# Where the state scan of a hybrid decoder runs: VectorE in two chains, or GpSimd in one

## The chip, the core and the metric

The kernel runs on one core of one Trainium2 chip. The metric is the device time of one execution in microseconds, the median of several runs. Five engines work side by side, each through its own queue in order: TensorE (PE; its weight loads are PEld), VectorE (DVE), ScalarE (ACT), GpSimd (POOL), and SyncE (SP), which only issues DMAs here.

## The reference

Two decoder layers over 256 positions of width 2048, in float32. Each layer projects the normed input, runs sliding-window attention and a state space model (S5) side by side, merges them through gates, and adds a gated feed-forward block. What matters here is the state space branch: 64 groups with 64 complex states each, advanced along the positions.

```python
def s5_ssm(u, lam_re, lam_im, log_dt, b_re, b_im, c_re, c_im, d_skip):
    ...
    bu_r = jnp.einsum('blgh,gph->blgp', uf, bbar_r)
    bu_i = jnp.einsum('blgh,gph->blgp', uf, bbar_i)
    ...
    _, _, s_r, s_i = lax.associative_scan(combine, (a_r, a_i, bu_r, bu_i), axis=1)
    y = (jnp.einsum('blgp,ghp->blgh', s_r, c_re) - jnp.einsum('blgp,ghp->blgh', s_i, c_im) + d_skip * uf)
    return y.reshape(B, L, SSM_WIDTH)
```

So s[t] = a * s[t-1] + (B u)[t] in complex numbers, a fixed for each state.

## The kernel before, in words

**Weights.** The kernel streams 475 MB of weights in pieces of up to 512 KB (128 x 4 x 256 numbers). The class Weights loads a piece by DMA, ScalarE rounds it to a high part `whi` (L106), VectorE forms the remainder `wlo = w - whi` (L121), and TensorE multiplies both parts with the activations (L295): 16 matmuls a piece, 8 with 512 columns and 8 with 256. High parts are made three pieces ahead, low parts two.

**The order of the work** is written out by hand. Every piece is one tick of the class Clock; side jobs are put on ticks with `later`, `at` and `stages`, and issued there into the queues of their engines. An engine works off its queue in order, so a waiting instruction holds up all behind it on that engine.

**The state space branch.** Two groups make a pair, whose 2 x 64 states fill 128 partitions; there are 32 pairs, real and imaginary. Two positions are joined into one step, so 256 positions give 128 columns c of the tile `S[128, 2, 32, 128]` (real/imaginary, pair, column). `states_in` (L735 to L748) fills all of S with the inputs of the steps, in eight ticks up to tick 37 (layer 0) and 24 (layer 1); ScalarE copies them out of PSUM (L748). Then `scan` (L759) makes 127 steps in place: for each column c, four products of the coefficients `scan_c` with column c - 1, and two sums into column c, for the real and the imaginary factor in turn. These are spread over ticks 39 to 109 in layer 0 and 26 to 109 in layer 1, one or two steps to a tick, in VectorE's queue between the `wlo` subtractions and the evictions. VectorE does each step in two halves of 16 pairs (two products at L766, four adds at L769), so that the two halves take turns.

**What uses the result.** At tick 110 `channels` starts: its matmuls `ys` (L963) read all columns of S. Their other operands `cb` and `ca` are cleared by GpSimd (L927, L928, issued at tick 91) and filled by ScalarE (L933, ticks 92 and 93).

**Other work in the same ticks.** Attention (`normed`, `attend`), the gate evictions (L343, L344, L896, L916, L943), and the weight stream. GpSimd has little: memsets of `prepare` (L649, L678), those of `cb` and `ca`, and a sum of squares at the very start (L412).

Of the kernel before, what the change touches and what calls it, by code (L numbers as in the profile page):

```python
# [10 lines left out]
F32 = mybir.dt.float32  # L11
# [7 lines left out]
P = 128  # L19
# [148 lines left out]
def build(ctx, tc, a, out):  # L168
    nc = tc.nc
    v, s, g, pe = nc.vector, nc.scalar, nc.gpsimd, nc.tensor  # L170
# [5 lines left out]
    tmp = ctx.enter_context(tc.tile_pool(name="tmp", bufs=1))  # L176
# [6 lines left out]
    def nm(x):  # L183
        uid[0] += 1
        return f"{x}_{uid[0]}"
# [372 lines left out]
    scan_c = cst.tile([P, L, 2, 2, 32], F32, name="scan_c")  # L558
# [146 lines left out]
    def layer(l, norm):  # L705
# [51 lines left out]
            at(v0 + n, states_in, n)  # L757

        def scan(first, last):  # L759

            S = hold["S"]
            for c in range(first, last):
                prs = [tmp.tile([P, 2, 2, 16], F32, name=nm("sc"), tag="sc", bufs=4) for _ in range(2)]
                fs = (slice(0, 16), slice(16, 32))
                for pr, f in zip(prs, fs):
                    v.tensor_mul(pr, scan_c[:, l, :, :, f], S[:, :, f, c - 1].unsqueeze(1).to_broadcast([P, 2, 2, 16]))  # L766
                for r in range(2):
                    for pr, f in zip(prs, fs):
                        v.tensor_add(S[:, :, f, c], S[:, :, f, c], pr[:, :, r, :])  # L769


        def c_times_a():
# [17 lines left out]
        for n in range(s0, s1):  # L790
            c = [1 + (P - 1) * (m - s0) // (s1 - s0) for m in (n, n + 1)]
            at(n, scan, *c)
# [389 lines left out]
```

## Time and profile before

| | |
|---|---|
| median of 3 runs | 2632.5 us (2630.88 to 2633.15) |
| the profiled execution's own time | 2632.42 us |
| its span | 2630.5 us |
| mean granted TensorE clock | 0.994 |
| busy: PE, PEld, DVE, ACT, POOL | 99%, 86%, 73%, 48%, 1% |
| HBM | 181 GB/s over the span |

The span is the time between the first and the last instruction of the profiled execution; its own time is 1.9 us longer. Matmuls overlap in their pipeline, so a busy PE need not be PE at its peak. The page also gives a chain of waits: from the last instruction back to what released each one. L numbers are lines of the kernel. A time in a stretch counts overlapping instructions once.

### The profile page before, as it was taken

The page shows a single profiled execution, that of the slowest core. Times are in us where ns is not written, and L with a number is a line of the kernel's source. Part 1 is how long each engine was busy: PE and PEld are TensorE (multiplying, and loading weights), DVE is VectorE, ACT ScalarE, POOL GpSimd, SP SyncE. Part 2 cuts the span into 40 slices and gives each one's busy share as a digit, 9 for nine tenths or more (in the row PEclk, how much of TensorE's full clock was granted, in tenths as well). Part 3 has the DMA queues.
Part 4 walks back from the last instruction along what each step waited for, and adds up shares of the span by engine and source line. Part 5 has one row for each costly group of instructions (what it writes and reads, how often), then busy time and mean ns, then how long its engine had stood idle before and what let it go on. Part 6 is the DMA issues. An engine that isn't in the chain of part 4 may idle for free.

```text
span 2630.5 us, 40564 instructions
## 1 busy us (share of the span) xinstructions
PE 2591.1 (99%) x15716; PEld 2259.7 (86%) x15716; DVE 1932.4 (73%) x3648; ACT 1267.8 (48%) x1725; POOL 29.0 (1%) x34
## 2 busy tenths in 40 slices
PE   7999899999999999999999999999999999999999
PEld 6878788888888888888888788888888888888888
DVE  8889997866765666566677999887666656665664
ACT  5666545544443444334455675465544434443442
POOL 2000000000000000000000000000000000000000
PEclk9999999999999999999999999999999999999999
DMA  6544455666655565566664445556656556655655
GB/s 203 169 129 144 145 170 164 200 209 194 203 172 191 190 189 179 192 199 187 199 201 160 141 149 170 178 173 211 213 185 187 183 199 188 190 186 187 188 180 172
DMA packets 139825, 477.85 MB, mean 182 GB/s; under 512 B 14960, under 2 KB 25456, under 8 KB 139632
## 3 DMA queue, kind: packets, MB, share of 16 engines
q1 hardware_dynamic: 139488, 475.06, 56.4%
q8 instruction: 123, 2.02, 0.3%
q14 instruction: 70, 0.57, 0.1%
q10 hardware_dynamic: 144, 0.20, 0.0%
HBM read 471.01 MB, written 4.19 MB: 181 GB/s over the span
## 4 chain that ended last, share of the span: by engine, by line
PE 81%; DVE 14%; ACT 3%; issue 1%; DMA 0%; SPq 0%; ACTq 0%; DVEq 0%
PE acc L295 79%; DVE wlo L121 5%; DVE S L769 3%; DVE sc L766 2%; ACT whi L106 1%; DVE wh L344 1%; DVE scs L855 1%; PE v L746 1%; PE ys L963 1%; ACT scs L869 1%; DVE ga L896 0%; DVE ga L916 0%; DMA w<-in_w_in 0%; PE acc L323 0%; PE bt L672 0%
## 5 line engine op out<-in xcount | busy, mean ns | idle before, releaser
L106 ACT CAST whi<-w 128x1024 fp32r<-128x1024 f32 (+1 forms) x881 | 910.6, 1047 | 769.6 <-PE acc L295 606.4
L121 DVE TENSOR_TENSOR wlo<-w,whi 128x1024 fp32r<-128x1024 f32 (+1 forms) x881 | 1061.4, 1219 | 221.2 <-ACT whi L106 220.2
L295 PE MATMUL acc<-h,whi 128*128 128x512 f32 x4448 | 1128.6, 396 | 0.8 <-DVE wh L344 0.8
L295 PEld LDWEIGHTS acc<-h,whi 128*128 128x128 f32 x4448 | 802.3, 189 | 156.8 <-issue 9.4
L295 PEld LDWEIGHTS acc<-h,wlo 128*128 128x128 f32 x4448 | 606.1, 190 | 53.5 <-DVE wlo L121 10.9
L295 PE MATMUL acc<-h,wlo 128*128 128x256 f32 x4448 | 621.8, 283 | 5.3 <-DVE wlo L121 5.3
L295 PE MATMUL acc<-hid,whi 128*128 128x512 f32 x1384 | 346.6, 392 | 0.0
L295 PEld LDWEIGHTS acc<-hid,whi 128*128 128x128 f32 x1384 | 248.9, 189 | 44.5
L337 DVE TENSOR_REDUCE j<-acc 128x512 f32<-128x1024 f32 x88 | 107.8, 1225 | 134.4 <-PE acc L295 134.4
L295 PEld LDWEIGHTS acc<-hid,wlo 128*128 128x128 f32 x1384 | 188.8, 190 | 13.5
L295 PE MATMUL acc<-hid,wlo 128*128 128x256 f32 x1384 | 193.0, 282 | 0.0
L1102 DVE TENSOR_TENSOR xn<-xn,acc 128x512 f32<-128x512 f32 x47 | 32.3, 688 | 173.5 <-PE acc L295 173.5
L769 DVE TENSOR_TENSOR S<-S,sc 128x32 f32<-128x32 f32 x1016 | 153.5, 222 | 0.0
L295 PE MATMUL acc<-mg,whi 128*128 128x512 f32 x512 | 128.2, 392 | 0.0
L766 DVE TENSOR_TENSOR sc<-scan_c,S 128x64 f32<-128x64 f32 x508 | 115.6, 269 | 0.0
L295 PEld LDWEIGHTS acc<-mg,whi 128*128 128x128 f32 x512 | 92.1, 189 | 16.5
L295 PE MATMUL acc<-yg,whi 128*128 128x512 f32 x384 | 96.2, 392 | 0.0
L295 PEld LDWEIGHTS acc<-yg,whi 128*128 128x128 f32 x384 | 69.1, 189 | 12.3
L295 PE MATMUL acc<-ya,whi 128*128 128x512 f32 x256 | 68.5, 410 | 10.0 <-DVE ya L161 6.0
L295 PEld LDWEIGHTS acc<-mg,wlo 128*128 128x128 f32 x512 | 69.8, 190 | 5.0
L351 ACT CAST hid<-j 128x512 fp32r<-128x512 f32 x44 | 27.4, 623 | 96.9 <-DVE j L1072 96.9
L295 PE MATMUL acc<-mg,wlo 128*128 128x256 f32 x512 | 71.4, 282 | 0.0
(238 smaller groups left out, 1500.7 us busy)
## 6 DMA issues: line engine op xcount, KB each, us to landing
w<-in_w_fi SPq DMA_DIRECT2D x352, 512.0 KB, 4.3
w<-in_w_in SPq DMA_DIRECT2D x207, 512.0 KB, 3.7
w<-in_w_fo SPq DMA_DIRECT2D x176, 512.0 KB, 4.4
w<-in_w_out SPq DMA_DIRECT2D x64, 512.0 KB, 4.4
w<-in_w_ab SPq DMA_DIRECT2D x32, 512.0 KB, 3.5
w<-in_w_sb SPq DMA_DIRECT2D x32, 512.0 KB, 4.1
w<-in_w_glu SPq DMA_DIRECT2D x16, 512.0 KB, 3.8
x<-in_x SPq DMA_DIRECT2D x8, 256.0 KB, 5.8
```

Of the source, the lines that this page charges most:

```text
L106: self.nc.scalar.copy(part[0][:, f, :], w[:, f, :])
L121: self.nc.vector.tensor_sub(lo[:, f, :], w[:, f, :], hi[:, f, :].bitcast(F32))
L295: pe.matmul(o, w, r, start=start, stop=last and j == m - 1 and lo_part == 1, skip_group_check=True)
L337: v.tensor_reduce(t, ps.rearrange("p s (a t) -> p s t a", a=2), axis=AX.X, op=ALU.add)
L344: v.tensor_add(t, t, ps[:, :, :T])
L351: s.copy(hi, src)
L746: pe.matmul(pss[r][:, c0 : c0 + P], bt[ri][o : o + 64, 2 * q4 + i, :], ur[o : o + 64, 2 * q4 + i, :], start=True, stop=True)
L766: v.tensor_mul(pr, scan_c[:, l, :, :, f], S[:, :, f, c - 1].unsqueeze(1).to_broadcast([P, 2, 2, 16]))
L769: v.tensor_add(S[:, :, f, c], S[:, :, f, c], pr[:, :, r, :])
L855: v.tensor_tensor_reduce(scs[b][:, f, :], scs[b][:, f, :], pv[:, f, :], 1.0, sk[:, b : b + 1], ALU.add, ALU.max, accum_out=mx[:, b, n : n ...
L869: s.activation(z, z, AF.Copy, scale=rd[:, b, n : n + 1])
L1102: v.tensor_add(t, t, ps[:, :, :T])
```

## The change

The scan's products and sums are issued on GpSimd (`g`) and no longer on VectorE (`v`), and each covers all 32 pairs: one product of 2 x 2 x 32 elements a partition and two adds of 2 x 32, where there were two products of 64 and four adds of 32. The product tile has two buffers. Where the steps stand among the ticks is not changed.

```diff
         def scan(first, last):
-
             S = hold["S"]
             for c in range(first, last):
-                prs = [tmp.tile([P, 2, 2, 16], F32, name=nm("sc"), tag="sc", bufs=4) for _ in range(2)]
-                fs = (slice(0, 16), slice(16, 32))
-                for pr, f in zip(prs, fs):
-                    v.tensor_mul(pr, scan_c[:, l, :, :, f], S[:, :, f, c - 1].unsqueeze(1).to_broadcast([P, 2, 2, 16]))
+                pr = tmp.tile([P, 2, 2, 32], F32, name=nm("sc"), tag="sc", bufs=2)
+                g.tensor_mul(pr, scan_c[:, l], S[:, :, :, c - 1].unsqueeze(1).to_broadcast([P, 2, 2, 32]))
                 for r in range(2):
-                    for pr, f in zip(prs, fs):
-                        v.tensor_add(S[:, :, f, c], S[:, :, f, c], pr[:, :, r, :])
+                    g.tensor_add(S[:, :, :, c], S[:, :, :, c], pr[:, :, r, :])
```

## Rows read from the trace of the kernel before

**Rows 1.** The page: busy time, share of the span and instructions of each engine, and the chain that ended last, its shares by engine and by line.
```profile
PE 2591.1 (99%) x15716; PEld 2259.7 (86%) x15716; DVE 1932.4 (73%) x3648; ACT 1267.8 (48%) x1725; POOL 29.0 (1%) x34
...
PE 81%; DVE 14%; ACT 3%; issue 1%; DMA 0%; SPq 0%; ACTq 0%; DVEq 0%
PE acc L295 79%; DVE wlo L121 5%; DVE S L769 3%; DVE sc L766 2%; ACT whi L106 1%; DVE wh L344 1%; DVE scs L855 1%; PE v L746 1%; PE ys L963 1%; ACT scs L869 1%; DVE ga L896 0%; DVE ga L916 0%; DMA w<-in_w_in 0%; PE acc L323 0%; PE bt L672 0%
```

**Rows 2.** Busy time by stretch, all engines: the two scan stretches, and one of 20 us in which nothing disturbs the weight loop. Columns: stretch, its length, busy us (and instructions) of each engine, granted clock, DMA share, GB/s.
```profile
150.00:402.00 252.00, 237.81 (x1420) 198.45 (x1423) 246.82 (x992) 144.11 (x278) 3.63 (x2) 0.97 0.48 151
1422.00:1696.00 274.00, 268.06 (x1642) 228.47 (x1641) 268.85 (x1017) 161.84 (x299) 3.63 (x2) 0.99 0.52 162
...
1340.00:1360.00 20.00, 20.00 (x116) 17.62 (x115) 13.92 (x20) 12.42 (x18) 0.00 (x0) 1.00 0.64 203
```

**Rows 3.** The same view for the matmuls of the weight loop (L295) alone: PE, PEld.
```profile
150.00:402.00 252.00, 214.79 (x1152) 180.66 (x1151) 0.97 0.48 151
...
1422.00:1696.00 274.00, 245.79 (x1354) 210.48 (x1353) 0.99 0.52 162
```

**Rows 4.** The timeline, in order of time: the last copy into S, the last adds of the scan and the first matmuls that read S, first of layer 0 and then of layer 1. Columns: start us, us, engine, line, operation, out<-in, count, idle time before and what ended it.
```profile
147.03 1.07 ACT L748 COPY S<-v 128x512 f32<-128x512 f32 x2 [2.06 <-PE v L746]
...
399.32 3.57 PE L963 MATMUL ys<-S,cb 128*32 128x127 f32 x64 [2.06 <-DVE S L769]
399.59 0.59 DVE L769 TENSOR_TENSOR S<-S,sc 128x32 f32<-128x32 f32 x4
...
1417.31 1.08 ACT L748 COPY S<-v 128x512 f32<-128x512 f32 x2 [1.59 <-PE v L746]
...
1693.90 0.60 DVE L769 TENSOR_TENSOR S<-S,sc 128x32 f32<-128x32 f32 x4
1693.97 1.98 PE L963 MATMUL ys<-S,cb 128*32 128x127 f32 x64
```

**Rows 5.** VectorE's groups by line and shape in 150 to 402 us, and below the "..." that ends them, two of 1422 to 1696 us. Columns: line, engine, operation, names, shapes, count | busy us, mean ns of one | idle time before.
```profile
L121 DVE TENSOR_TENSOR wlo<-w,whi 128x1024 fp32r<-128x1024 f32 x73 | 88.8, 1217 | 1.0 <-ACT whi L106 1.0
L769 DVE TENSOR_TENSOR S<-S,sc 128x32 f32<-128x32 f32 x508 | 76.7, 221 | 0.0
L766 DVE TENSOR_TENSOR sc<-scan_c,S 128x64 f32<-128x64 f32 x254 | 57.8, 269 | 0.0
...
L896 DVE TENSOR_TENSOR ga<-wh,rms 128x512 f32<-128x512 f32 x8 | 5.5, 692 | 0.3
L916 DVE TENSOR_TENSOR ga<-ga,wh 128x512 f32<-128x512 f32 x8 | 5.5, 692 | 0.3
L943 DVE TENSOR_TENSOR gs<-gs,rms 128x512 f32<-128x512 f32 x5 | 3.5, 693 | 0.2
...
L809 DVE SCALAR_TENSOR_TENSOR q<-q,qg,qrs 128x512 f32<-128x512 f32 x2 | 1.5, 752 | 0.1
...
L375 DVE SCALAR_TENSOR_TENSOR qrs<-rs,rs 128x512 f32<-128x512 f32 x2 | 1.4, 692 | 0.1
...
L121 DVE TENSOR_TENSOR wlo<-w,whi 128x1024 fp32r<-128x1024 f32 x85 | 103.4, 1217 | 0.2 <-issue 0.2
...
L809 DVE SCALAR_TENSOR_TENSOR q<-q,qg,qrs 128x512 f32<-128x512 f32 x4 | 3.0, 752 | 0.1
```

**Rows 6.** The timeline of 19 to 26 us: GpSimd's adds of 512 elements, each reading the sum of the one before, and VectorE's instructions beside the last of them. Columns as in rows 4.
```profile
19.58 1.27 POOL L412 TENSOR_TENSOR ssq<-ssq,sq 128x512 f32<-128x512 f32 x1
20.92 1.27 POOL L412 TENSOR_TENSOR ssq<-ssq,sq 128x512 f32<-128x512 f32 x1
...
23.54 1.21 DVE L121 TENSOR_TENSOR wlo<-w,whi 128x1024 fp32r<-128x1024 f32 x1
23.61 2.27 POOL L412 TENSOR_TENSOR ssq<-ssq,sq 128x512 f32<-128x512 f32 x1
...
24.68 1.27 DVE L455 TENSOR_SCALAR cw<-cw 128x64 f32<-128x64 f32 x1
```

**Rows 7.** GpSimd's other operations: two of the timeline (columns as in rows 4; the second reads what the first wrote), and two groups by line and shape (columns as in rows 5).
```profile
2.09 0.24 POOL L268 IOTA ndist<- 128x128 f32 x1
2.40 0.29 POOL L270 TENSOR_SCALAR_AFFINE_SELECT ndist<-ndist 128x128 f32<-128x128 f32 x1
...
L649 POOL MEMSET pw<- 128x2048 f32 x4 | 7.1, 1816 | 317.2 <-PE acc L295 317.2
...
L678 POOL MEMSET k<- 128x1024 f32 x2 | 1.9, 963 | 0.0
```

**Rows 8.** The timeline near 36 us, when GpSimd is idle: a VectorE product of 64 neighbouring elements a partition.
```profile
35.88 0.22 DVE L569 TENSOR_TENSOR cw<-params,cw 128x64 f32<-128x64 f32 x1
```

**Rows 9.** The timeline of layer 0: GpSimd's memset of `cb` and ScalarE's first copies into it.
```profile
259.28 1.81 POOL L927 MEMSET cb<- 128x2048 f32 x1 [227.64 <-PE sc L850]
...
342.56 2.51 ACT L933 COPY cb<-cc 64x512 f32<-64x512 f32 x4
```

**Rows 10.** TensorE by the microsecond around a wait of layer 0. Columns: stretch, its length, PE busy us (and matmuls), granted clock, DMA share, GB/s.
```profile
280.00:281.00 1.00, 0.37 (x2) 1.00 0.04 16
...
283.00:284.00 1.00, 0.00 (x0) 0.75 0.68 164
284.00:285.00 1.00, 0.82 (x2) 0.50 0.70 279
...
290.00:291.00 1.00, 1.00 (x8) 0.83 0.64 66
```

## The prediction

> **What bounds the kernel now.** I first read the busy line and the chain that ended last [rows 1]: TensorE is busy nearly all the time, yet the chain also passes through VectorE, the two scan lines L766 and L769 among it. A mean hides where, so I next cut the span into stretches. The scan of layer 0 lies in 150 to 402 us and that of layer 1 in 1422 to 1696 us; there VectorE is busy for 246.8 of 252 us and 268.9 of 274 us, while GpSimd does two memsets [rows 2]. So VectorE is full in the two scan stretches, and only there.
>
> What would TensorE need alone? In an undisturbed stretch it does 116 matmuls of the weight loop in 20 us [rows 2]. The 1152 and 1354 of L295 [rows 3] then take 198.6 and 233.4 us. The other matmuls add 237.8 - 214.8 = 23.0 us and 268.1 - 245.8 = 22.3 us [rows 2, 3]. The floors are 221.6 and 255.7 us against 252 and 274: a scan that vanished could give back 30.4 + 18.3, nearly 49 us, and no more.
>
> The scan ends as it is needed: in layer 0 the last add ends at 400.2 us, and the first `ys` matmul had waited 2.06 us for the scan; in layer 1 the end is at 1694.5 us. The states are complete far earlier, when the last copy into S ends: 148.1 and 1418.4 us [rows 4].
>
> **What is removed.** 127 steps per layer of two multiplies and four adds on VectorE: 76.7 + 57.8 = 134.5 us in layer 0 [rows 5], and the same in layer 1. Half of VectorE's work in these stretches goes; what stays (112 and 134 us) is no bound.
>
> **What is added: the price of a step.** On GpSimd a step is a multiply of 128 elements and two adds of 64, each needing the one before it. No such operation is in the trace, so I build it. The nearest row is the add of 512 elements, 1.27 us where no other instruction of length held it; the next of that dependent chain starts 1.34 us after it [rows 6], so dependence costs 0.07 us, as between the iota at 2.09 us and the select at 2.40 that reads it [rows 7]. For the fixed part I take the select: 0.29 us, less 128 elements at the memsets' slope (1816 - 963) / 1024 = 0.833 ns [rows 7], leaves 0.18 us. Then one element of an add costs (1.27 - 0.18) / 512 = 2.13 ns, a multiply 0.45 us, an add 0.32 us, and a step 0.45 + 2 x 0.32 + 3 x 0.07 = 1.30 us.
>
> That is for neighbouring elements. S[..., c] steps over 128 elements, and VectorE shows a price for this: its scan multiply of 64 takes 269 ns [rows 5] against 0.22 us for a contiguous 128x64 product [rows 8], so 0.77 ns per element with one strided operand. Its strided add of 32 takes 221 ns; by VectorE's slope, (1217 - 220) / 960 = 1.04 ns, a contiguous one would take 187, so 1.06 ns per element with a strided read and write. Charged on GpSimd: 128 x 0.77 + 2 x 64 x 1.06 = 0.23 us. The step is **1.53 us**, my estimate, and 127 of them 194 us.
>
> The ends: without any dependence gap, with the memset's fixed part (963 - 1024 x 0.833 = 110 ns) and no charge for strides, a step is 0.40 + 2 x 0.26 = 0.91 us. With every element at twice 2.13 ns it is 0.73 + 2 x 0.45 + 0.21 = 1.84 us. I take 1.53 because the stride is certain and VectorE's rows price it.
>
> [...]
>
> **What is added: VectorE in its way.** While a `wlo` subtraction ran (23.54, 1.21 us) the GpSimd add issued beside it lasted 2.27 instead of 1.27 us: 1.00 us lost, 0.21 us hidden under its own start. The VectorE operation behind (24.68, 64 elements) took 1.27 us instead of some 0.22 [rows 6, 8]: it sat out the GpSimd add. So GpSimd and these VectorE instructions take turns. I charge GpSimd 1.00 us for each `wlo`, 73 in layer 0 and 85 in layer 1, and 0.69 - 0.21 = 0.48 us for each other long VectorE operation that reads two tensors in SBUF. These are 8 + 8 + 5 (L896, L916, L943) in each layer and four lines from L809 to L375 with 2 each in layer 0 and 4 in layer 1, so 29 and 37 [rows 5]. That is 73 + 14 = 87 us and 85 + 18 = 103 us. At zero it is a rival (below); VectorE itself has room for its share of the waiting.
>
> **What is moved past what.** No DMA moves. GpSimd's queue holds, ahead of the last steps, the memsets of `cb` and `ca`, 1.8 us each, 3.6 us a layer. Their place is clock tick 91: 94 steps of layer 0 stand before it, 33 behind. Before, they ran as soon as buffers came free, at 259.3 us; the ScalarE copies into `cb` come at 342.6 [rows 9]. In my forecast GpSimd gets through 94 steps (144 us), some 65 us of turns and the memsets at 148 + 144 + 65 + 4 = 361 us, and ScalarE stands at L933 until then, with the `whi` casts behind it, then `wlo`, then TensorE. During such a stall no `wlo` is made, so GpSimd runs undisturbed: a stall here moves no work, it only divides the lateness between L933 and the `ys` matmuls. The sum needs only the end of the scan.
>
> **The sum.** Layer 0: 148.1 + 194.3 + 87 + 3.6 = 433.0, against 400.2: 33 us later. Layer 1: 1418.4 + 194.3 + 103 + 3.6 = 1719.3, against 1694.5: 25 us later. Everything behind `ys` shifts with it: +58 us. After a gap of 3.8 us in TensorE's work the granted clock stood at 0.50 (1.2 GHz) until about 290 us, some 7 us from its fall [rows 10]; a long wait ahead of `ys` costs half of that, 3.5 us, once per layer (behind L933 TensorE has slack): +7 us. In all +65 us on the profiled execution, whose own 2632.4 us is the median of 2632.5 to 0.1 us: **2697 us**.
>
> As a rule: change = 254 x step - 331 us (the constant is both starts, turns and memsets less both old ends). It is zero at a step of **1.30 us**, the price without strides. That is why the chance is not higher.
>
> **The rivals.**
> (a) *GpSimd's step is under 1.30 us* and the scan ends before TensorE asks. The mechanism is the same, at L769; for it, the fixed part may be 0.11 us and dependent starts may overlap; against it, the strides. At 1.15 us layer 0 gains 15 us and layer 1 its whole 18: 2599 us. Faster.
> (b) *The turns cost GpSimd nothing*, as when VectorE's operand reads fit into GpSimd's fixed times. Then 194 + 4 us hide under both floors, and TensorE is the bound: 2632 - 49 = 2584 us. Against it stands the 2.27 us row. [...]
> (c) *The strides are dearer than twice*: a step over 1.84 us, +143 us and more, 2776 us upward.
> (d) *No measurable change*: a step between 1.28 and 1.32 us.
>
> **How the numbers follow.** Forecast 0.65, (a) 0.17, (b) 0.08, (c) 0.04, (d) 0.06. Faster is (a) and (b), 0.25; same 0.06; slower 0.69. 0.2% is 5 us, about what a measurement of this kernel can tell from no change. The range starts at (a)'s 2600, leaving out (b), and ends at the 1.84 us step, 2776. The likeliest case alone spans 2650 to 2776.
>
> **What would show it.** Right: VectorE's busy time falls by 134 us in each stretch; GpSimd is busy throughout it; its multiplies last 0.55 and its adds 0.39 us, with about 1 us more where a `wlo` runs; ScalarE's longest waits are at L933 for a GpSimd memset, and TensorE waits for L769 ahead of `ys`, in both layers. Wrong in size: a spacing of steps away from 1.5 us between two `wlo`. Wrong in kind: GpSimd idle before the `ys` matmuls, or its operations no longer beside a `wlo` than away from one.

## The result: 1% slower, where 2.5% was forecast

The changed kernel takes 2658.1 us (2656.9 to 2658.9) against 2632.6: 25.5 us more, a ratio of 1.0098 with the interval 1.008 to 1.0115. The forecast was 2697 us, +65. The direction and the range held; the size is two and a half times too large.

The page after: busy time of the engines, and the chain that ended last.
```profile
PE 2583.5 (97%) x15716; PEld 2260.5 (85%) x15716; DVE 1751.0 (66%) x2124; ACT 1268.5 (48%) x1725; POOL 513.5 (19%) x796
...
PE 43%; issue 36%; POOL 19%; DVE 2%; ACT 1%; DMA 0%; SPq 0%; POOLq 0%
PE acc L295 41%; POOL S L765 12%; POOL sc L763 7%; PE ys L959 1%; DVE wlo L121 1%; PE acc L323 0%; ACT whi L106 0%; DMA w<-in_w_in 0%; ACT h L390 0%; ACT sq L404 0%; POOL cb L923 0%; POOL pw L649 0%; POOL cb L924 0%; DVE ur L729 0%; DVE u L719 0%
```
VectorE's scan lines have left the chain of rows 1, its share is 2% and no longer 14%, and GpSimd has 19% of the span: 12% + 7% of 2655 us are 504 us, most of both scans from end to end. ("issue" is time for which the profile shows nothing that the engine waited for, so this chain is a sign of where to look and not a sum.)

The two scan stretches by engine (columns as in rows 2):
```profile
148.00:415.00 267.00, 229.77 (x1392) 197.59 (x1394) 156.69 (x231) 148.14 (x282) 237.46 (x381) 0.93 0.46 144
1418.00:1720.00 302.00, 287.53 (x1780) 246.42 (x1782) 192.60 (x269) 176.90 (x321) 253.53 (x383) 0.97 0.49 156
```
VectorE, full before [rows 2], is idle for 110 us of each; GpSimd is the busy one.

The timeline of the ends of the scans, layer 0 and then layer 1 (columns as in rows 4; a row with x2 holds both adds of a step):
```profile
147.93 0.54 POOL L763 TENSOR_TENSOR sc<-scan_c,S 128x128 f32<-128x128 f32 x1 [116.51 <-ACT S L748]
...
414.46 1.07 PE L959 MATMUL ys<-S,cb 128*32 128x127 f32 x16 [13.99 <-POOL S L765]
415.08 0.80 POOL L765 TENSOR_TENSOR S<-S,sc 128x64 f32<-128x64 f32 x2
...
1434.70 0.80 POOL L763 TENSOR_TENSOR sc<-scan_c,S 128x128 f32<-128x128 f32 x1 [818.85 <-ACT S L748]
...
1716.50 1.07 PE L959 MATMUL ys<-S,cb 128*32 128x127 f32 x16 [6.66 <-POOL S L765]
1717.13 0.80 POOL L765 TENSOR_TENSOR S<-S,sc 128x64 f32<-128x64 f32 x2
```
In layer 0 the scan runs from 147.9 to 415.9 us, 268 us, and ends 15.7 us later than before [rows 4]. In layer 1 it starts 16 us later, takes 283 us and ends at 1717.9 us, 23.4 us later than before. That is nearly all of the 24.6 us by which the span grew.

Who waited for GpSimd, in the chain of waits of 140 to 440 us and then of 1400 to 1740 us (us in total, times, longest):
```profile
ACT cb L929 <- POOL cb L923: 28.5, 1, 28.5
PE ys L959 <- POOL S L765: 14.4, 2, 14.0
...
ACT cb L929 <- POOL cb L923: 12.7, 1, 12.7
PE ys L959 <- POOL S L765: 7.1, 2, 6.7
```
These are the two places that the prediction named, in both layers.

### The profile page after: what moved, and what is told of

Its sections match the earlier page's. It is cut to its first block, busy times and chain, and to the rows that moved or that the text cites. A ratio compares the mean times of both kernels' runs of the same rounds, so it can differ in the third digit from the quotient of the medians.

```text
span 2655.1 us, 39807 instructions
## 1 busy us (share of the span) xinstructions
PE 2583.5 (97%) x15716; PEld 2260.5 (85%) x15716; DVE 1751.0 (66%) x2124; ACT 1268.5 (48%) x1725; POOL 513.5 (19%) x796
## 4 chain that ended last, share of the span: by engine, by line
PE 43%; issue 36%; POOL 19%; DVE 2%; ACT 1%; DMA 0%; SPq 0%; POOLq 0%
PE acc L295 41%; POOL S L765 12%; POOL sc L763 7%; PE ys L959 1%; DVE wlo L121 1%; PE acc L323 0%; ACT whi L106 0%; DMA w<-in_w_in 0%; ACT h L390 0%; ACT sq L404 0%; POOL cb L923 0%; POOL pw L649 0%; POOL cb L924 0%; DVE ur L729 0%; DVE u L719 0%
## 5 line engine op out<-in xcount | busy, mean ns | idle before, releaser
L121 DVE TENSOR_TENSOR wlo<-w,whi 128x1024 fp32r<-128x1024 f32 (+1 forms) x881 | 1085.7, 1251 | 255.7 <-ACT whi L106 254.9
L295 PE MATMUL acc<-h,whi 128*128 128x512 f32 x4448 | 1132.8, 397 | 26.4 <-ACT whi L106 26.3
L295 PEld LDWEIGHTS acc<-h,whi 128*128 128x128 f32 x4448 | 805.4, 190 | 183.2 <-ACT whi L106 26.7
L295 PEld LDWEIGHTS acc<-h,wlo 128*128 128x128 f32 x4448 | 607.8, 191 | 53.1 <-DVE wlo L121 9.7
L295 PE MATMUL acc<-h,wlo 128*128 128x256 f32 x4448 | 621.7, 283 | 7.4 <-DVE wlo L121 7.4
L763 POOL TENSOR_TENSOR sc<-scan_c,S 128x128 f32<-128x128 f32 x254 | 183.0, 720 | 954.9 <-ACT S L748 935.4
L295 PE MATMUL acc<-hid,whi 128*128 128x512 f32 x1384 | 346.5, 392 | 0.0
L765 POOL TENSOR_TENSOR S<-S,sc 128x64 f32<-128x64 f32 x508 | 301.9, 594 | 39.8
L295 PEld LDWEIGHTS acc<-hid,whi 128*128 128x128 f32 x1384 | 248.9, 189 | 44.5
L295 PEld LDWEIGHTS acc<-hid,wlo 128*128 128x128 f32 x1384 | 188.8, 190 | 13.5
L295 PE MATMUL acc<-hid,wlo 128*128 128x256 f32 x1384 | 193.0, 282 | 0.0
L295 PE MATMUL acc<-mg,whi 128*128 128x512 f32 x512 | 128.2, 392 | 0.0
L295 PEld LDWEIGHTS acc<-mg,whi 128*128 128x128 f32 x512 | 92.1, 189 | 16.5
L295 PE MATMUL acc<-yg,whi 128*128 128x512 f32 x384 | 96.1, 392 | 0.0
L295 PEld LDWEIGHTS acc<-yg,whi 128*128 128x128 f32 x384 | 69.1, 189 | 12.3
L295 PEld LDWEIGHTS acc<-mg,wlo 128*128 128x128 f32 x512 | 69.8, 190 | 5.0
L295 PE MATMUL acc<-mg,wlo 128*128 128x256 f32 x512 | 71.4, 282 | 0.0
L390 ACT ACTIVATE h<-xn,params 128x256 fp32r<-128x256 f32 x48 | 21.9, 503 | 98.8 <-DVE xn L1046 66.1
```

Source lines behind the costliest of these rows:

```text
L121: self.nc.vector.tensor_sub(lo[:, f, :], w[:, f, :], hi[:, f, :].bitcast(F32))
L295: pe.matmul(o, w, r, start=start, stop=last and j == m - 1 and lo_part == 1, skip_group_check=True)
L390: s.activation(self.h[:, k, 0, :], x[:, r, :], AF.Copy, scale=self.gain[:, k : k + 1])
L763: g.tensor_mul(pr, scan_c[:, l], S[:, :, :, c - 1].unsqueeze(1).to_broadcast([P, 2, 2, 32]))
L765: g.tensor_add(S[:, :, :, c], S[:, :, :, c], pr[:, :, r, :])
```

## The experiments

The medians of all runs, and the ratio to the kernel before on the same chip:

| kernel | us | ratio | 95% interval |
|---|---|---|---|
| before: VectorE, two chains | 2632.6 | | |
| changed: GpSimd, one chain | 2658.1 | 1.0098 | 1.008 to 1.0115 |
| e1: changed, `wlo` by a one-input instruction | 2592.1 | 0.9849 | 0.9832 to 0.9865 |
| e7: before, `wlo` by a one-input instruction | 2630.9 | 0.9995 | 0.9986 to 1.0005 |
| e2: VectorE, one chain | 2656.4 | 1.0092 | 1.0076 to 1.0107 |
| e3: GpSimd, two chains | 2685.2 | 1.0202 | 1.0187 to 1.0218 |
| e4: changed, `cb` and `ca` cleared by VectorE | 2656.1 | 1.0092 | 1.0077 to 1.0107 |
| e8: half of the pairs on each engine | 2657.0 | 1.0097 | 1.0082 to 1.0112 |
| e5: changed, S by column | 2659.1 | 1.0104 | 1.0089 to 1.012 |
| e6: before, S by column | 2642.7 | 1.0042 | 1.0027 to 1.0057 |
| e9: before, two pairs of S side by side | 2604.5 | 0.9894 | 0.9877 to 0.991 |
| e10: changed, two pairs of S side by side | 2621.3 | 0.9956 | 0.9941 to 0.9971 |

### Are the turns real? (e1, e7)

```diff
-self.nc.vector.tensor_sub(lo[:, f, :], w[:, f, :], hi[:, f, :].bitcast(F32))
+with self.nc.allow_low_precision(reason="a copy"):
+    self.nc.vector.tensor_reduce(lo[:, f, :], hi[:, f, :].bitcast(F32).unsqueeze(3), axis=AX.X, op=ALU.add)
```


> The changed kernel, but VectorE makes the low part of a weight piece by an instruction of equal length with one input: a reduction of `whi` over an axis of length 1 in place of w - whi. The low parts then hold the high parts, so the remainder of the weights is left out. Theory (GpSimd's scan ends when its 127 steps of 1.467 us, its memsets and the turns that it loses to VectorE's two-input instructions have been paid; in the changed kernel the turns are 78 us in layer 0 and 93 us in layer 1, some 63 and 73 of them from `wlo`): the GpSimd operations beside a `wlo` last no longer than the others, the scan of layer 0 takes 205 to 215 us in place of 268 and ends before TensorE asks for it, no engine waits for GpSimd, and the time is 2580 to 2600 us. Rival 1 (GpSimd's own step is the whole lateness, the turns are only how the records look): the scan still takes 250 us or more and the time stays within 10 us of 2658. Rival 2 (any VectorE instruction holds GpSimd up, whatever it reads): likewise 2658.

> The control of the first experiment: the kernel before, scan on VectorE, with the low part of a weight piece made from `whi` alone (a reduction over an axis of length 1), so the remainder of the weights is left out. Theory (the 66 us that this gave the changed kernel were GpSimd's turns): without GpSimd beside it there is nothing to gain, VectorE is as full as before, and the time is 2622 to 2640 us. Rival (the one-input instruction makes the weight stream easier by itself): 2590 to 2610 us.

With GpSimd's scan the time falls by 66 us, to 2592; with VectorE's scan the same edit changes nothing (2630.9, within the interval). So it is not the weight stream that became easier. What a turn looks like in the changed kernel: a `wlo` and the GpSimd add beside it (timeline at 285 us), and below the "..." all `wlo` of the first scan (columns as in rows 5):
```profile
284.36 1.38 DVE L121 TENSOR_TENSOR wlo<-w,whi 128x1024 fp32r<-128x1024 f32 x1
284.75 1.23 POOL L765 TENSOR_TENSOR S<-S,sc 128x64 f32<-128x64 f32 x1
...
L121 DVE TENSOR_TENSOR wlo<-w,whi 128x1024 fp32r<-128x1024 f32 x73 | 99.8, 1390 | 16.2 <-ACT whi L106 16.2
```
And in e1, beside a `wlo` of about the same time and then at the end of the scan:
```profile
281.60 2.34 DVE L122 TENSOR_REDUCE wlo<-whi 128x1024 fp32r<-128x1024 f32 x2
282.16 0.83 POOL L766 TENSOR_TENSOR S<-S,sc 128x64 f32<-128x64 f32 x2
...
351.23 0.82 POOL L766 TENSOR_TENSOR S<-S,sc 128x64 f32<-128x64 f32 x2
```
Beside a two-input `wlo` an add lasts 1.23 us, alone 0.36; beside a one-input instruction of the same length two adds take 0.83 together. In e1 the scan of layer 0 ends at 352 us after 205 us, no engine waits for it, and TensorE alone sets the time. Both rivals fall: without the turns the scan is 63 us shorter, and a VectorE instruction of the same length does not always hold GpSimd up. e1 takes the second input in SBUF away from `wlo` and changes the operation along with it, so which of the two frees GpSimd it does not show. A pair of the same operation stands 0.7 us apart in e1 (timeline at 280 us):
```profile
280.20 0.82 POOL L766 TENSOR_TENSOR S<-S,sc 128x64 f32<-128x64 f32 x2
280.27 0.69 DVE L345 TENSOR_TENSOR wh<-wh,acc 128x512 f32<-128x512 f32 x1 [1.77 <-ACT wh L344]
280.99 0.69 DVE L913 TENSOR_TENSOR ga<-ga,wh 128x512 f32<-128x512 f32 x1
281.10 0.99 POOL L764 TENSOR_TENSOR sc<-scan_c,S 128x128 f32<-128x128 f32 x1
```
Beside the first, whose second input `acc` lies in PSUM, two adds take 0.82 us; beside the second, which reads two tensors in SBUF, a product takes 0.99 us, elsewhere 0.53. The number of inputs does not settle it either: in [rows 6] a `TENSOR_SCALAR` that reads one tensor took 1.27 us beside a GpSimd add. From 268 to 205 us is 63 us for the 73 `wlo` of the stretch: **0.86 us each**. In layer 1 the scan takes 207.5 us in place of 283.2, which is 0.89 us for each of 85.

### The engine or the shape of the chain? (e2, e3)

e2 is the changed kernel with `v.tensor_mul` and `v.tensor_add` in place of `g.`; e3 is the kernel before with `g.` in place of `v.`.

> The changed kernel's single chain of all 32 pairs, put back on VectorE: the engine is undone, the chain's shape is kept. Theory (the engine makes the whole difference): three dependent instructions of about 0.38, 0.29 and 0.29 us replace six interleaved ones that take 1.06 us a step together; a step takes 0.9 to 1.1 us, and the time is 2615 to 2640 us. Rival (two interleaved halves are what makes the scan fast, on any engine): a step takes 1.3 us or more and the time is above 2660.

> The scan on GpSimd, but in the two interleaved chains of 16 pairs that the kernel before has: six instructions a step and not three. Theory (a GpSimd instruction is mostly fixed cost, and a dependent start costs only 0.07 us): about 0.35 us for a multiply of 64 and 0.27 for an add of 32, so 1.8 us a step without VectorE in its way in place of 1.467, and 254 x 0.33 = 84 us more than the change: 2720 to 2760 us. Rival (waiting for the result before is what a GpSimd step consists of, and a second chain hides it): the step is 1.4 us or less and the time 2658 or less.

Here my theory fell. One chain on VectorE takes 2656 us, as long as on GpSimd: of the two edits in the change, the shape alone costs 24 us on VectorE, and once it is made the engine costs nothing more that these runs can tell. The two equal times are made of different things, waiting for results on VectorE, steps and turns on GpSimd; with two chains (e3 and the kernel before) the engine costs 53 us. The timeline shows what the shape costs on VectorE; first the kernel before, then e2:
```profile
299.88 0.45 DVE L766 TENSOR_TENSOR sc<-scan_c,S 128x64 f32<-128x64 f32 x2
300.25 0.60 DVE L769 TENSOR_TENSOR S<-S,sc 128x32 f32<-128x32 f32 x4
300.76 0.45 DVE L766 TENSOR_TENSOR sc<-scan_c,S 128x64 f32<-128x64 f32 x2
```
```profile
404.63 0.37 DVE L763 TENSOR_TENSOR sc<-scan_c,S 128x128 f32<-128x128 f32 x1
405.04 0.60 DVE L765 TENSOR_TENSOR S<-S,sc 128x64 f32<-128x64 f32 x2
405.68 0.40 DVE L763 TENSOR_TENSOR sc<-scan_c,S 128x128 f32<-128x128 f32 x1
```
Six interleaved instructions take 0.88 us a step, since each starts before the last has ended (the second product at 300.06 us, while the first, of 0.27 us, runs to 300.15); three dependent ones take 1.05 us, since each waits for the last (the first add at 405.04 us, 0.04 behind the end of the product). 127 x 0.17 = 22 us more on a full engine, of which layer 0 passes on 12.7 (its last add ends at 412.9 and not 400.2 us). The rival's step of 1.3 us was not there either.

On GpSimd it is the other way round. e3's step away from VectorE:
```profile
335.43 0.64 POOL L766 TENSOR_TENSOR sc<-scan_c,S 128x64 f32<-128x64 f32 x2
336.03 0.91 POOL L769 TENSOR_TENSOR S<-S,sc 128x32 f32<-128x32 f32 x4
336.90 0.64 POOL L766 TENSOR_TENSOR sc<-scan_c,S 128x64 f32<-128x64 f32 x2
```
It is 1.47 us for six instructions, the same as for three: both halves of my expectation were off. The extra instructions cost (2 x 0.33 + 4 x 0.26 = 1.70 us of records, where the three have 0.52 + 2 x 0.36 = 1.24), and the overlap gives as much back. Yet e3 is 27 us slower than the change, and its scan of layer 0 ends at 428.6 us and not 415.9. The means of its instructions over layer 0 (to 440 us), and below them those of the changed kernel (to 416 us):
```profile
L769 POOL TENSOR_TENSOR S<-S,sc 128x32 f32<-128x32 f32 x508 | 168.6, 366 | 0.0
L766 POOL TENSOR_TENSOR sc<-scan_c,S 128x64 f32<-128x64 f32 x252 | 119.1, 492 | 0.0
```
```profile
L765 POOL TENSOR_TENSOR S<-S,sc 128x64 f32<-128x64 f32 x254 | 146.5, 577 | 19.9
L763 POOL TENSOR_TENSOR sc<-scan_c,S 128x128 f32<-128x128 f32 x127 | 88.3, 695 | 126.3 <-ACT S L748 116.5
```
Over the durations alone (0.26 and 0.33 us; 0.36 and 0.52 us) the excess is 508 x 0.106 + 252 x 0.162 = 95 us in e3 and 254 x 0.217 + 127 x 0.175 = 77 us in the change. So the turns are dearer for many overlapping instructions. Why, no run shows.

### Is the wait at L929 a cost of its own? (e4)

```diff
-            g.memset(cb, 0.0)
-            g.memset(ca, 0.0)
+            v.memset(cb, 0.0)
+            v.memset(ca, 0.0)
```


> The changed kernel with the two memsets of `cb` and `ca` on VectorE and not on GpSimd, where they stand behind 94 of 127 steps and ScalarE waits for them 28.5 us in layer 0 and 12.7 us in layer 1. Theory (GpSimd's chain is the bound from start to end, and a stall at L929 only divides its lateness): ScalarE no longer waits there, TensorE runs on to `ys` and waits there for the whole lateness, some 35 us in layer 0; the time falls only by the memsets' own 3.6 us a layer, to 2645 to 2656 us. Rival (the wait behind the memsets is a cost of its own): it falls by 28 + 13 us to about 2617.

ScalarE's 28.5 us wait is gone, and the time falls by 2 us, to just above the theory's 2645 to 2656. The wait turned up ahead of `ys` (chain of waits of 140 to 440 us):
```profile
PE ys L959 <- POOL S L765: 40.7, 2, 40.3
```
14 + 28 became 40 us. The wait at L929 was worth nothing, because GpSimd's chain went on during it: from 333 to 353 us of the changed kernel GpSimd is busy for 17.4 of 20 us, VectorE for none. The memsets' own 3.6 us a layer did not come back either: the scan of layer 0 takes 267.2 us in place of 268.0, and a GpSimd product takes 3.47 us beside VectorE's memsets instead (timeline; alone it takes 0.52 us; in layer 1 it is the same, 3.48 us):
```profile
319.34 3.47 POOL L763 TENSOR_TENSOR sc<-scan_c,S 128x128 f32<-128x128 f32 x1
```
It starts just ahead of the second memset (319.58 us) and ends behind the first `wlo` after it. Beside the first memset a product took 0.53 us and two adds 0.82, hardly longer than elsewhere, so what held this one through the second is open.

### Both engines at once (e8)

Against the kernel before:
```diff
-                prs = [tmp.tile([P, 2, 2, 16], ...) for _ in range(2)]
-                ...
+                for e, f, tag in ((v, slice(0, 16), "sv"), (g, slice(16, 32), "sg")):
+                    pr = tmp.tile([P, 2, 2, 16], F32, name=nm("sc"), tag=tag, bufs=2)
+                    e.tensor_mul(pr, scan_c[:, l, :, :, f], S[:, :, f, c - 1].unsqueeze(1).to_broadcast([P, 2, 2, 16]))
+                    for r in range(2):
+                        e.tensor_add(S[:, :, f, c], S[:, :, f, c], pr[:, :, r, :])
```


> The scan divided by pairs: one chain of 16 pairs on VectorE, one of the other 16 on GpSimd, both at the same places of the order. Theory (GpSimd is bound by steps and turns, VectorE by its own work and by waiting for GpSimd's reads): GpSimd alone would need about 1.06 us a step, 135 us a layer, and with turns of some 80 to 100 us ends near TensorE's floor; VectorE keeps half of the scan, about 67 us a layer on top of 112 to 134, and waits up to 0.3 us in front of each of its 381 scan instructions, 57 us or more: 236 to 260 us a layer, so the time is 2610 to 2660 us, no clear gain on the kernel before. Rival 1 (both engines work side by side, since half of each one's instruction is not at the memory): 2590 to 2600 us. Rival 2 (every turn costs both engines a whole instruction): above 2680 us.

2657 us, within the theory's interval, and 26 us slower than the kernel before: half of the scan has left VectorE, and nothing is gained. In layer 0 GpSimd's half ends at 347 us and VectorE's at 410.5, so VectorE's is the one that counts. VectorE's adds while GpSimd's half runs (150 to 347 us), then when it has ended (348 to 411 us), and three rows of the timeline near the end:
```profile
L767 DVE TENSOR_TENSOR S<-S,sc 128x32 f32<-128x32 f32 x172 | 55.1, 320 | 5.9
L767 DVE TENSOR_TENSOR S<-S,sc 128x32 f32<-128x32 f32 x81 | 17.7, 218 | 2.8
...
408.94 0.27 DVE L765 TENSOR_TENSOR sc<-scan_c,S 128x64 f32<-128x64 f32 x1
409.25 0.47 DVE L767 TENSOR_TENSOR S<-S,sc 128x32 f32<-128x32 f32 x2
409.75 0.27 DVE L765 TENSOR_TENSOR sc<-scan_c,S 128x64 f32<-128x64 f32 x1
```
The turns cost VectorE too: its adds take 320 ns beside GpSimd's half and 218 without it, its products 368 and 271. But they are not the whole reason. Even undisturbed, half a step on VectorE takes 0.81 us (408.94 to 409.75), because its three instructions wait for each other as in e2; the whole step of two interleaved halves took 0.88 us. Half of the scan thus holds VectorE for 127 x 0.81 = 103 us a layer, not for the 67 that I expected, and without any turns this split would have given back only 127 x 0.07 = 9 us a layer.

### What do the strides cost? (e5, e6, e9, e10)

```diff
-                hold["S"] = p32("S", [P, 2, 32, P])
+                hold["S"] = p32("S", [P, P, 2, 32]).rearrange("p c r q -> p r q c")
```


> The changed kernel with S laid out by column, so that the 64 numbers of a column lie side by side for the scan; ScalarE's copies into S and the `ys` matmuls step over 64 numbers in place of 1. Theory (each strided number costs GpSimd extra, about 0.23 us a step by the prediction's charge, and the sum of steps and turns sets the end): a step away from VectorE's instructions falls from 1.467 us to 1.20 to 1.30 us, the scan ends 20 to 35 us earlier in each layer, layer 0 gains on the kernel before, layer 1 reaches TensorE's floor, and the time is 2600 to 2625 us. Rival 1 (strides cost GpSimd nothing; its step is fixed cost and 3 ns an element): a step stays at 1.42 us or more and the time within 10 us of 2658. Rival 2 (the strided `ys` matmuls or copies cost what the scan gains): the step falls, and the time does not.

> The kernel before (two chains on VectorE) with S laid out by column. Theory (VectorE is the bound of the two scan stretches of the kernel before): its multiplies fall from 269 to about 220 ns and its adds from 222 to about 190 ns, a step of six from 0.88 us to about 0.75 us, 16 us less per layer on a full engine: 2590 to 2615 us. Rival 1 (what VectorE pays is the start of each instruction, and the strides hide in it): the step stays at 0.85 us or more and the time at 2625 to 2635. Rival 2 (the strided `ys` matmuls or copies eat it): the step falls and the time does not.

In both, rival 2 won. First e5, a step of GpSimd away from VectorE and a group of `ys` matmuls (timeline); then such a group of the kernel before. Both groups run at the granted clock of 1.00:
```profile
340.90 0.46 POOL L763 TENSOR_TENSOR sc<-scan_c,S 128x128 f32<-128x128 f32 x1
341.44 0.72 POOL L765 TENSOR_TENSOR S<-S,sc 128x64 f32<-128x64 f32 x2
342.24 0.46 POOL L763 TENSOR_TENSOR sc<-scan_c,S 128x128 f32<-128x128 f32 x1
...
409.08 7.38 PE L959 MATMUL ys<-S,cb 128*32 128x127 f32 x64
```
```profile
406.32 1.95 PE L963 MATMUL ys<-S,cb 128*32 128x127 f32 x64
```
GpSimd's step falls from 1.47 to 1.34 us (340.90 to 342.24). TensorE's 256 matmuls of a layer now read every 64th number, and in layer 0 go from 9.4 to 27.8 us, overlaps counted once. (The 34 and 12 us that e9's expectation gives for them count overlapping matmuls twice.) The scan of layer 0 ends 15 us earlier than in the changed kernel, at 400.8 us, and `ys` takes back 18. So the strides cost GpSimd 0.13 us a step; the prediction charged 0.23. In e6 VectorE's products fall from 269 to 218 ns and its adds from 222 to 191, the scan of layer 0 ends at 382.0 and not 400.2 us, and `ys` takes 27.5 us: the time rises by 11 us. ScalarE's copies into S also take longer, 1.12 in place of 0.59 us each.

In e9 and e10 two neighbouring pairs lie side by side in each column, and `ys` steps over 2 numbers (the copies, the products and the sums get the matching views of `S`):
```diff
-                hold["S"] = p32("S", [P, 2, 32, P])
+                hold["S"] = p32("S", [P, 2, 2, 8, P, 2])     # e9; e10: [P, 2, 16, P, 2]
...
-                            dst, src = (..., S[:, ri, pr, :]) if odd else (..., S[:, ri, pr, 0 : P - 1])
+                            dst, src = (..., S[:, pr // 16, ri, pr % 16 // 2, :, pr % 2]) if odd else (...)
```


> The kernel before (two chains on VectorE), with S laid out so that two neighbouring pairs lie side by side in each column: the scan meets runs of two numbers, and the `ys` matmuls and ScalarE's copies step over 2 numbers, where the layout by column had them step over 64. Theory (in the layout by column the scan ended 17 us earlier in each layer, and the `ys` matmuls took 34 us a layer in place of 12): if TensorE and ScalarE read and write at a step of 2 nearly as at 1, the gain stays and the loss goes: the scan's multiplies take 218 to 235 ns and its adds 190 to 205 ns, and the time is 2595 to 2615 us, under both kernels. Rival 1 (any step but 1 slows the `ys` matmuls): each layer loses up to 22 us there again, 2630 to 2645. Rival 2 (VectorE needs longer runs): the multiplies stay at 260 ns or more and the time at 2632.

> The changed kernel with the same layout, two neighbouring pairs side by side. Theory (GpSimd's end is steps plus turns; by column a step was 1.34 us and not 1.467, and the scan of layer 0 ended 16 us earlier): if runs of two are enough for GpSimd and TensorE, the step is 1.33 to 1.40 us and each layer loses 10 to 16 us less than the change: 2622 to 2642 us, about the kernel before. Rival 1 (GpSimd gains by wholly contiguous columns only): the step stays at 1.45 us or more, 2655 to 2660. Rival 2 (the step of 2 slows the `ys` matmuls): the scan ends earlier and the time does not fall.

The theory holds in both. e9: the scan's instructions by minimum, median and maximum ns, and a group of `ys` matmuls of layer 0:
```profile
L770 DVE TENSOR_TENSOR S<-S,sc x1016: 181/192/205, 151.9 to 1660.0; 128x32 f32<-128x32 f32 x170
L766 DVE TENSOR_TENSOR sc<-scan_c,S x508: 214/220/230, 151.6 to 1659.5; 128x64 f32<-128x64 f32 x170
...
386.25 2.03 PE L964 MATMUL ys<-S,cb 128*32 128x127 f32 x64
```
Runs of two serve VectorE as well as whole columns (220 and 192 ns, in e6 218 and 191), and TensorE hardly notices a step of 2 (2.03 us a group in place of 1.95). e9 is 28 us faster than the kernel before and 54 us faster than the changed one: the version that beats both. In e10 GpSimd's step is 1.34 us too:
```profile
332.68 0.46 POOL L763 TENSOR_TENSOR sc<-scan_c,S 128x128 f32<-128x128 f32 x1
...
334.02 0.46 POOL L763 TENSOR_TENSOR sc<-scan_c,S 128x128 f32<-128x128 f32 x1
```
With it the GpSimd scan ends at 400.0 us, beside 400.2 for VectorE's old layout, and the kernel is 11 us under the one before. The prediction put the threshold at a step of 1.30 us; with the measured turns of 78 and 93 us it lies at (331 + 19) / 254 = 1.38, so 1.34 is on the faster side of it.

## Why the prediction was wrong, step by step

**What bounds the kernel, and where the waits come: right.** VectorE was full; GpSimd takes its place as the bound; ScalarE stands at L929 and TensorE ahead of `ys`, in both layers. That a stall at L929 only divides the lateness was right (e4). Rival (b), turns at no cost, is out: the turns were worth 66 us or more (e1, where TensorE takes over as the bound). In the changed kernel an add took 1.23 us beside a `wlo` and 0.36 us alone.

One sign of being right did not come. VectorE's busy time in the stretch of layer 0 fell by 90 us (246.8 to 156.7), not by 134. The 134.5 us add two groups of records that overlap: at 0.88 us a step the scan had held VectorE for 127 x 0.88 = 112 us. And the `wlo` became longer by the turns, 1390 and not 1217 ns, 13 us for 73. Nothing in the sum hangs on this reading.

**The terms of the sum: every one too large.** The step in a stall of the changed kernel:
```profile
405.67 0.52 POOL L763 TENSOR_TENSOR sc<-scan_c,S 128x128 f32<-128x128 f32 x1
406.26 0.79 POOL L765 TENSOR_TENSOR S<-S,sc 128x64 f32<-128x64 f32 x2
407.13 0.52 POOL L763 TENSOR_TENSOR sc<-scan_c,S 128x128 f32<-128x128 f32 x1
...
408.60 0.52 POOL L763 TENSOR_TENSOR sc<-scan_c,S 128x128 f32<-128x128 f32 x1
```

| term | forecast | measured | too much, both layers |
|---|---|---|---|
| a step away from VectorE | 1.53 us | 1.467 us (405.67 to 408.60 is two steps of 1.465) | 254 x 0.063 = 16 us |
| turns, layer 0 and 1 | 87 and 103 us | 268 - 186.3 - 3.6 = 78; 283.2 - 186.3 - 3.6 = 93 | 19 us |
| clock after the wait ahead of `ys` | 3.5 us a layer | 16.2 - 15.7 = 0.5 us in layer 0, 24.57 - 23.43 = 1.1 in layer 1 | about 5 us |

In the last row 16.2 and 24.57 us are the lateness of the second group of `ys` matmuls (422.54 against 406.32, 1723.89 against 1699.32), and 15.7 and 23.43 that of the end of the scan.

Together 40 us: 65 forecast, 24.6 in the span. The **step that failed is the price of a turn**, the largest of the three: I charged 1.00 us for each `wlo` by the single row of 2.27 us [rows 6], and e1 prices a turn at 0.86. In that row GpSimd's add had started 0.07 us behind the `wlo`; in the pair shown at e1 GpSimd's record starts some 0.4 us behind VectorE's (284.36 and 284.75), and the `wlo` is itself longer, 1.38 us. Whether this is why a turn costs less there, no run shows. The other turns were about right: without those of `wlo`, e1's scans leave 205.3 - 186.3 - 3.6 = 15 and 207.5 - 186.3 - 3.6 = 18 us, and 14 and 18 were charged. That these other operations take turns no row of the kernel before shows, so the 0.48 us for each were my estimate; in e1 the products beside two `ga<-ga,wh` took 0.99 us (281.10) and 1.08 us (284.58), 0.46 and 0.55 more than the 0.53 elsewhere.

The second is the stride within the step, 0.13 us in place of 0.23 (e5); the rest of the step was 0.04 us dearer than charged, 1.34 and not 1.30.

The third is the clock. It does fall during the wait ahead of `ys` (in layer 0 it was granted 0.79 in the microsecond from 402 us and 0.50 from 403, `ys` began at 414.5), but in layer 0 it did so in the kernel before as well (0.78 from 399 us, 0.50 from 400), whose wait was only 2 us. TensorE by the microsecond, changed and then before, in layer 0 and below the "..." in layer 1 (columns as in rows 10):
```profile
418.00:419.00 1.00, 1.00 (x17) 0.50 0.08 16
...
1718.00:1719.00 1.00, 1.00 (x20) 0.50 0.00 0
```
```profile
400.00:401.00 1.00, 1.00 (x26) 0.50 0.86 328
...
1694.00:1695.00 1.00, 1.00 (x37) 1.00 0.70 213
```
In layer 0 both kernels ran the first `ys` at a granted clock of 0.50, so the term was paid already. (The trace gives this clock as a share of full speed; the 1.2 GHz of the prediction is not in it.) In layer 1 the kernel before ran it at 1.00 and the changed one at 0.50, and the term is real; but it came to 1.1 us and not 3.5. About half of the time at the lower level went by while TensorE still waited for the scan: by the microsecond the granted clock was 0.65 from 1713 us and 0.50 from 1714, `ys` began at 1716.5, and the clock was back at 0.94 from 1720 and 1.00 from 1721.

**Why 4 to 16% became a factor of 2.6.** The step was 4% too dear and the turn of a `wlo` 16%. The forecast was 254 x step - 331 us: two numbers near 390 and 330 of which only the difference shows. An error of 0.06 us in a step is 16 us. The rule stated that zero lies at 1.30 us; what it lacked is a thought for errors of one sign in all terms, which add up.

## What to carry to other kernels

Before moving work from VectorE to GpSimd, count the instructions that stay on VectorE, and look in a trace at how long a GpSimd instruction takes beside one of them: here each `wlo`, which reads two tensors in SBUF, cost GpSimd 0.86 us and became 0.17 us longer itself, so an idle GpSimd beside a busy VectorE was not spare capacity. Where a change moves work and reshapes it, price the new shape on the old engine first: one dependent chain cost 24 us on VectorE alone. Where a forecast is a small difference of large terms, take each term from the middle of its range and ask of each whether the kernel before pays it already. And look first at what the operands cost where they are: laying two pairs side by side gave 28 us with no engine changed.

## What the runs showed of the hardware

- A GpSimd product of 128 numbers took 0.52 us and an add of 64 took 0.36 us at a step of 512 bytes; 0.46 and 0.32 us with runs of two numbers or with whole columns.
- Dependent GpSimd instructions started 0.07 us behind the end of the last; independent ones 0.03 to 0.04 us ahead of it (e3: spacings of 0.30 and 0.22 us for records of 0.33 and 0.26). Six short ones and three long ones took the same 1.47 us.
- On VectorE a step of six interleaved instructions took 0.88 us, one of three dependent instructions of twice the size 1.05 us (e2), and one of three dependent instructions of the same size, half the work, 0.81 us (e8).
- A VectorE `tensor_tensor` of 1024 numbers cost the scan on GpSimd 0.86 us, a `tensor_reduce` of the same length nothing that shows (e1: two adds beside it took 0.83 us, away from VectorE 0.79).
- A group of 64 `ys` matmuls of 127 or 128 columns took 1.95 us at a granted clock of 1.00 with neighbouring numbers, 2.03 us with every second one (e9), and 6.3 to 7.4 us with every 64th (e6).
